# The sums of a mixture of experts: rows added in DRAM, or carried to their tokens by TensorE

## The chip, the cores and the metric

The kernel runs on one core of a Trainium2 chip. The metric is the device time of one execution in microseconds (us). Engines are named as in the profile: PE is TensorE, DVE is VectorE, ACT is ScalarE, POOL is GpSimd, and SP issues most of the transfers. SBUF is the working memory on the chip, PSUM holds the sums of PE in banks of 128 x 512 float32, and DRAM lies outside.

## What is computed

One decoder block for 512 tokens of 1024 channels, all in float32. A layer norm, two parallel token mixers and a second layer norm give `h`. Then each token is sent to the 4 of 32 experts that its router scores highest. The last part of the reference, cut:

```
top_logit, top_e = lax.top_k(h @ w_router + b_router, 4)
top_w = softmax(top_logit)
# for each token t and each of its four experts e:
hgu  = h[t] @ w_gate_up[e] + b_gate_up[e]            # 1024 x 2048
gate = minimum(hgu[:1024], 7); up = clip(hgu[1024:], -7, 7)
act  = (up + 1) * gate * sigmoid(1.702 * gate)
y[t] += top_w * (act @ w_down[e] + b_down[e])        # 1024 x 1024
ple = sigmoid(h @ w_ple_gate) * (p @ w_ple_proj)
out = layer_norm(2 ** 0.25 * h + y + ple)
```

The sum `2 ** 0.25 * h + y + ple`, a table of 512 x 1024 float32 (2 MB), is what the change is about.

## The kernel before

The mixers and the output projection come first. Their products are F32R (float32 in a single pass), each value split into a high and a low part, three products for one (`split_parts`, `mm3`, lines 168 to 184). From about 670 us on the experts run.

The experts are sorted on the chip by how many tokens chose them. Experts at odd places from 7 on are **short**, with 64 slots; the others are **long**, with 64 + 32 slots (`BLOCKS`, `IS_SHORT`, line 45). That makes 13 short and 19 long ones. An expert's weights are 12 loads of 1 MB: eight for gate and up, four for down. `unit` (line 1311) puts the loads into a ring of 18 tiles of 1 MB, made of buffers that the mixers no longer need. Two of the 18 are the two halves of `hr`, which holds `h` after the second norm. SP issues the loads; a load waits until PE has used the tile's last content.

In `expert` (line 1454) PE multiplies the gathered tokens by the weights as float32 products (two records each in the trace). The tokens are the stationary side: 64 slots fill half of the columns of the array, 32 slots a quarter. So `products` (line 1442) issues two or four products side by side, which write to different partitions of one bank, as a "block" whose row of partitions holds a half or a quarter of the channels. `pg` takes gate and up of the first 64 slots, `pq` of the other 32; four of the eight input pieces are held back (`LATE`) so that the gating on ACT and DVE (lines 1500 to 1504) runs beside the rest. The results are transposed (`turned`) and multiplied by the down weights into `po` and `pq`.

**Sums.** `y_d` is a table in DRAM. `scaled_rows` (line 1237) writes `2 ** 0.25 * h` into it by way of a tile `tmp`; the sort of the experts uses a tile of the same tag (line 1130). At the end of each expert ACT multiplies `po` and `pq` by the slots' weights into `og` (line 1587), and POOL issues one or two indirect transfers that add the rows to `y_d` at the slots' tokens (line 1596). The embedding term is worked out in 32 pieces of 128 tokens by 128 channels, one or two in each expert (`embed`, line 1024); after each four, POOL issues a transfer of 256 KB that adds them to `y_d` (line 1044).

**The end.** The last expert is short; its table is filled up so that all its 64 slots hold a token, and the rows of these tokens are finished apart from the others. While its weights are used, SP reads all of `y_d` back into four tiles (`fetch_rows`, line 1358), which waits for all adds, and POOL reads the last expert's own rows into `yr` (line 1402). The fourth load of its down weights is held behind `fetch_rows` (line 1570). `norm_steps` (line 1371) norms the four tiles in small steps between the products; two of them are finished on POOL. The last expert's own rows get their sum from `po` on DVE and their norm in `last_rows` (line 1411), and are written over the output by an indirect transfer.

The order of instructions on each engine is made by a planner from the program's order, with some pairs kept as written (`keep_in_program_order`) and some loads held back (`issue_after`). Short sums and transposes share four PSUM banks (tag `att`); `pg` and `pq` of the up products use four others.

Of the kernel before, what the change touches and what calls it, by code (L numbers as in the profile page):

```python
# [14 lines left out]
U8 = mybir.dt.uint8  # L15
AF = mybir.ActivationFunctionType
ALU = mybir.AluOpType
# [49 lines left out]
FETCH_AT = 3  # L67
# [28 lines left out]
def block_kernel(ctx: ExitStack, tc: tile.TileContext, a: dict, out: bass.AP):  # L96
# [704 lines left out]
    row_add = rtc.tile([P, 4], F32, name="row_add")  # L801
    key = rtc.tile([P, NE], F32, name="key")
# [8 lines left out]
    def routing_setup():  # L811
# [6 lines left out]

        v_.memset(row_add, 0.0)
# [61 lines left out]
    def table_rows(pool, ohs, ne, gi, si, parts):  # L881
        rows_from(pool, picked(pool, ohs, ne, lambda n, e: ids[:, n, :], 3), gi, si, parts)
# [8 lines left out]
    def tables(pool, e0, ne, base, gi, si, ws, places):  # L891
        ohs = pool.tile([P, NT, ne, P], BF16, name="ohs", tag="ohs")
        for n in range(NT):
            one_hot_slots(ohs, n, e0, ne, base, places)
        table_rows(pool, ohs, ne, gi, si, False)
        table_weights(pool, ohs, e0, ne, 1, ws)
# [127 lines left out]
    def embed(i):  # L1024
# [18 lines left out]
        if n == NT - 1:  # L1043
            nc.gpsimd.dma_start(y_d[:S, cs].rearrange("(n q) c -> q n c", q=P), emb["out"], accum_op=ALU.add)
# [125 lines left out]
    def first_tables():  # L1170
# [14 lines left out]
        table_rows(rtc, ohs0, 4, pair(gidx, 0), pair(sidx, 0), True)  # L1185
# [15 lines left out]
    def main_tables(e0):  # L1201
# [10 lines left out]
        weights_from(tb[:, :, 3:], pair(wslot, e0))  # L1212

# [94 lines left out]
    units += [hr[:, 2 * i:2 * i + 2, :].rearrange("p j d -> p (j d)") for i in range(2)]  # L1308
# [49 lines left out]
    def fetch_rows():  # L1358
        for n in range(NT):
            fetched = nc.sync.dma_start(yts[n], y_d[n * P:(n + 1) * P, :])  # L1360
        return fetched

# [8 lines left out]
    def norm_steps():  # L1371
        got = {}

        def first(n):
            mean, rs = got[n] = row_stats(ep, yts[n], keep=keep, bufs=NT + 1)
# [4 lines left out]
        def second(n):  # L1380
            if n in POOL_ROWS:
                shift, rs = got[n]
                keep(s_.activation(yts[n], yts[n], AF.Identity, scale=rs, bias=shift))
                g_.tensor_tensor(yts[n], yts[n], gb3, op=ALU.mult)
                g_.tensor_tensor(yts[n], yts[n], lasts["bias"], op=ALU.add)
            else:
                normed(yts[n], yts[n], got[n], gb3, lasts["bias"], keep)
# [66 lines left out]
    def expert(e):  # L1454
# [52 lines left out]
        down_order = (0, 2, 1, 3) if last else range(4)  # L1507
        if last:

            raws = [unit(rows_up(k)) for k in range(KD)]  # L1510
            raws_down = [unit(rows_down(u)) for u in down_order[:FETCH_AT]]
            yr = rows_to_add_to(e)
            fetched = fetch_rows()
            norm_steps()
        late = []
        for k in range(KD):
# [4 lines left out]
            raw = raws[k] if last else unit(rows_up(k))  # L1521
# [30 lines left out]
        if e == NE - 1:  # L1552
            spread(lasts["bias"], a["ln_moe_b"][0])

# [4 lines left out]
        if not last:  # L1559
            turned(sgs, as_, (more or [first])[0], range(2) if more else range(2, 4), True)  # L1560
# [3 lines left out]
        for i, u in enumerate(down_order):  # L1564
            if not last:
                raw = unit(rows_down(u))
            elif i < FETCH_AT:
                raw = raws_down[i]
            else:
                with tc.issue_after(fetched.ins):  # L1570
                    raw = unit(rows_down(u))
            if last and i == 1:
                turned(sgs, as_, first, range(2, 4), True)
# [107 lines left out]
```

## Time and profile before

| | us |
|---|---|
| median of three runs | 1806.24 |
| lowest and highest | 1805.43 to 1811.08 |
| the profiled execution | 1799.9 |
| its span, first to last instruction | 1798.2 |
| PE busy in the span | 1722.1 (96%) |
| DVE, ACT, POOL busy | 557.7, 409.5, 196.6 |
| mean granted PE clock | 0.985 of full |

The profile is of one execution, so its rows add up to its own time and not to the median. Busy time of PE is made of records whose ends are modelled: several products can run side by side, and a record can lie over the next one. What counts is how far starts lie from each other. A wait in a row stands in brackets: how long the engine was idle before it, and what released it.

### The profile page before, as it was taken

What the parts mean: (1) busy time and instruction counts of PE and PEld (TensorE: products, weight loads), DVE (VectorE), ACT (ScalarE), POOL (GpSimd) and SP (SyncE); (2) the same over time, 40 slices, a digit from 0 to 9 for tenths busy, and PEclk for the clock granted to TensorE, in tenths of its full rate; (3) what the DMA queues carried; (4) which work ended last, traced back from release to release, by engine and by line L of the source; (5) the groups of instructions that cost most, each with busy time, mean ns of one, the idle gap of its engine ahead of it and who ended that gap; (6) DMA issues with size and microseconds to landing.
All of it is one profiled execution on the core that took longest, in us unless ns stands there. A gap on an engine that the chain in (4) does not pass through costs nothing. (4 is left out here: it accounts for less than half of the span.)

```text
span 1798.2 us, 26077 instructions
## 1 busy us (share of the span) xinstructions
PE 1722.1 (96%) x10591; PEld 985.3 (55%) x10591; DVE 557.7 (31%) x1326; ACT 409.5 (23%) x653; POOL 196.6 (11%) x202
## 2 busy tenths in 40 slices
PE   6999999999998999999999999999999999999994
PEld 5888887788886873334334543443443443434422
DVE  7566455436344654102112112112111111112004
ACT  3665355234322321011110101111111011001111
POOL 1000000000000101111111110110110111110113
PEclk9999999999999999999999999999999999999997
DMA  8322233322217487999999999999999999999993
GB/s 268 106 71 71 71 132 103 141 94 71 94 71 288 168 332 283 370 366 387 364 342 361 412 408 384 405 411 386 406 412 372 405 412 371 405 385 413 404 355 133
DMA packets 127642, 513.93 MB, mean 286 GB/s; under 512 B 14434, under 2 KB 44546, under 8 KB 78228
## 3 DMA queue, kind: packets, MB, share of 16 engines
q1 hardware_dynamic: 95988, 466.11, 64.8%
q0 software_dynamic: 16160, 29.63, 6.8%
q10 hardware_dynamic: 15360, 16.39, 2.7%
q8 instruction: 86, 1.41, 0.3%
q14 instruction: 48, 0.39, 0.1%
HBM read 484.36 MB, written 27.72 MB: 285 GB/s over the span
## 5 line engine op out<-in xcount | busy, mean ns | idle before, releaser
L1452 PE MATMUL pg<-raw,turned 128*64 128x512 f32 (+1 forms) x2120 | 424.9, 533 | 6.1 <-DVE up L1502 3.7
L1452 PEld LDWEIGHTS pg<-raw,turned 128*64 128x64 f32 x2120 | 162.1, 137 | 227.5 <-issue 178.4
L1502 DVE TENSOR_SCALAR up<-pg 128x256 f32<-128x256 f32 (+1 forms) x45 | 24.2, 537 | 732.1 <-PE pg L1452 732.1
L1452 PE MATMUL pq<-raw,turned 128*32 128x512 f32 (+1 forms) x2000 | 192.1, 498 | 0.0
L1452 PE MATMUL po<-raw,turned 128*64 128x512 f32 x784 | 178.4, 604 | 0.0
L182 PE MATMUL proj<-H,parts_w 128*128 128x512 f32 x640 | 157.4, 394 | 3.4 <-ACT vt L499 2.0
L182 PE MATMUL proj<-parts_w,H 128*128 128x512 f32 x640 | 159.7, 394 | 0.0
L174 DVE TENSOR_TENSOR parts_w<-raw,parts_w 128x1024 fp32r<-128x1024 f32 x84 | 102.5, 1222 | 153.0 <-ACT parts_w L172 152.5
L1500 ACT ACTIVATE sgs<-pg 128x256 f32<-128x256 f32 (+1 forms) x45 | 21.3, 474 | 544.9 <-PE pg L1452 544.9
L182 PEld LDWEIGHTS proj<-H,parts_w 128*128 128x128 f32 x640 | 119.1, 188 | 28.3 <-ACT vt L499 2.4
L182 PEld LDWEIGHTS proj<-parts_w,H 128*128 128x128 f32 x640 | 120.1, 189 | 24.8 <-DVE H L939 0.3
L1596 POOL DMA_INDIRECT y_d<-og,sidx x50 | 80.3, 1605 | 455.8 <-ACT og L1587 260.3
L172 ACT ACTIVATE parts_w<-raw 128x1024 fp32r<-128x1024 f32 x84 | 88.7, 1059 | 177.4 <-PE proj L184 158.0
L1452 PEld LDWEIGHTS pq<-raw,turned 128*32 128x32 f32 x2000 | 54.8, 109 | 120.0 <-issue 101.7
L1452 PEld LDWEIGHTS po<-raw,turned 128*64 128x64 f32 x784 | 55.8, 140 | 99.3 <-issue 96.1
L1326 POOL DMA_INDIRECT xg<-h_d,gidx x49 | 50.6, 1032 | 393.4 <-PE ptr L1342 346.2
L184 PE MATMUL proj<-parts_w,H 128*128 128x512 f32 x320 | 83.5, 391 | 0.0
L184 PE MATMUL proj<-H,parts_w 128*128 128x512 f32 x320 | 80.5, 390 | 0.0
L1587 ACT ACTIVATE og<-po,wslot 128x512 f32<-128x512 f32 x32 | 22.0, 687 | 213.8 <-PE po L1452 213.8
L184 PEld LDWEIGHTS proj<-parts_w,H 128*128 128x128 f32 x320 | 60.3, 189 | 12.6
L184 PEld LDWEIGHTS proj<-H,parts_w 128*128 128x128 f32 x320 | 59.9, 188 | 12.4
L1037 PE MATMUL ple<-rawg,H 128*128 128x128 f32 x512 | 62.4, 275 | 0.0
(351 smaller groups left out, 1808.1 us busy)
## 6 DMA issues: line engine op xcount, KB each, us to landing
raw<-in_w_gate_up_dram SPq DMA_DIRECT2D x223, 1024.0 KB, 19.8
raw<-in_w_down_dram SPq DMA_DIRECT2D x98, 1024.0 KB, 19.4
raw<-in_w_in_dram SPq DMA_DIRECT2D x36, 1024.0 KB, 4.9
hr<-in_w_gate_up_dram SPq DMA_DIRECT2D x22, 1024.0 KB, 20.1
hr<-in_w_down_dram SPq DMA_DIRECT2D x20, 1024.0 KB, 19.5
gb<-in_w_gate_up_dram SPq DMA_DIRECT2D x11, 1024.0 KB, 19.7
gb<-in_w_down_dram SPq DMA_DIRECT2D x10, 1024.0 KB, 20.1
raw<-in_w_proj_a_dram SPq DMA_DIRECT2D x4, 1024.0 KB, 5.2
```

The source lines that it names most:

```text
L172: s_.activation(hi, src, AF.Copy)
L174: v_.tensor_tensor(lo, src, f32(hi), op=ALU.subtract)
L182: t_.matmul(ps, wh if keep else x, x if keep else wh, start=st, stop=False)
L184: t_.matmul(ps, wl if keep else xh, xh if keep else wl, start=False, stop=stop)
L1037: t_.matmul(pg[:, :P], H2[:, k, t], emb["gate"][:, k, :], start=(k == 0), stop=(k == KD - 1))
L1326: g_.indirect_dma_start(out=columns_of(xg, i), out_offset=None, in_=by_parts(h2_d, parts), in_offset=bass.IndirectOffsetOnAxis(ap=gidx[:, ...
L1452: t_.matmul(dst, x, cols, start=start, stop=stop, skip_group_check=closed)
L1500: s_.activation(dst, gate, AF.Sigmoid, scale=SW_ALPHA)
L1502: v_.tensor_scalar(tmp, up, LIMIT + 1.0, 1.0 - LIMIT, op0=ALU.min, op1=ALU.max)
L1587: s_.activation(columns_of(og, i), (po, pq)[i][:, :D // parts] if i else po, AF.Copy, scale=wslot[:, e, i:i + 1])
L1596: g_.indirect_dma_start(out=by_parts(y_d, parts), out_offset=rows_of(e, i), in_=columns_of(og, i), in_offset=None, compute_op=ALU.add)
```

## The change

`y_d` is no longer used in the main path. `hr` keeps the sums: it is scaled in place, the embedding's pieces are added to it by DVE, and each expert's weighted rows are carried to their tokens by PE. For that `tokens_held` makes, with the tables, the token number of each slot (`holds`; three columns, one for the first 64 slots and two for the other 32, of which each is valid in one half of the partitions). `weighted` splits the weighted rows into a high and a low part. `add` compares a row of token numbers with `holds` into `mine`, a matrix of slots by tokens, and multiplies it by both parts, with 64 slots in each half of the partitions. DVE adds the four sums to `hr`. The two halves of this work (256 tokens each) are queued in `waiting` and taken up in the next expert, behind the second and the fourth piece of its up products.

The ring of weights has 16 tiles, since `hr` is in use. In the last expert `fetch_rows` is gone, the norms read `hr`, its loads are issued in the ordinary order, and `yr` is picked from `hr` by a float32 product with a choice matrix. The scratch space of POOL's transfers is set to 8192 bytes. The path for overfull experts, which these inputs don't take, writes `hr` to `y_d` first.

```diff
+    holds = rtc.tile([P, NE, 3], F32, name="holds")
+    skip = rtc.tile([P, 2], F32, name="skip")
+    token_i = rtc.tile([P, S], I16, name="token_i")
...
+    def tokens_held(tb, e0):
+        hd = rtc.tile([P, 4], F32, name="hd")
+        v_.tensor_tensor(hd, tb[:, :, 0], tb[:, :, 1], op=ALU.add)
+        v_.scalar_tensor_tensor(hd, tb[:, :, 2], 2.0 * S, hd, op0=ALU.mult, op1=ALU.add)
+        hv = hd.rearrange("p (e i) -> p e i", i=2)
+        v_.tensor_scalar(holds[:, e0:e0 + 2, 0], hv[:, :, 0], -2.0 * S, None, op0=ALU.add)
+        for i in range(2):
+            v_.tensor_scalar(holds[:, e0:e0 + 2, 1 + i], hv[:, :, 1], skip[:, i:i + 1], -2.0 * S, op0=ALU.add, op1=ALU.add)
...
         v_.tensor_tensor(dst, pg[:, P:2 * P], dst, op=ALU.mult)
-        if n == NT - 1:
-            nc.gpsimd.dma_start(y_d[:S, cs].rearrange("(n q) c -> q n c", q=P), emb["out"], accum_op=ALU.add)
+        v_.tensor_tensor(hr[:, n, cs], hr[:, n, cs], dst, op=ALU.add)
...
         for n in range(NT):
-            tmp = ep.tile([P, D], F32, name="tmp", tag="og")
-            s_.activation(tmp, hr[:, n, :], AF.Copy, scale=ALPHA)
-            nc.scalar.dma_start(y_d[n * P:(n + 1) * P, :], tmp)
-        nc.scalar.dma_start(y_d[S:], hr[:, 0, :])
+            s_.activation(hr[:, n, :], hr[:, n, :], AF.Copy, scale=ALPHA)
...
-    units += [hr[:, 2 * i:2 * i + 2, :].rearrange("p j d -> p (j d)") for i in range(2)]
...
     def rows_to_add_to(e):
-        yr = ep.tile([P, D // 2], F32, name="yr", tag="xg")
-        g_.indirect_dma_start(out=yr, out_offset=None, in_=by_parts(y_d, 2), in_offset=rows_of(e, 0))
+        both = ep.tile([P, D], F32, name="yr", tag="xg")
+        yr, oh = both[:, :D // 2], both[:, D // 2:D // 2 + NT * SHORT_CAP].rearrange("p (n m) -> p n m", n=NT)
+        py = psm.tile([P, 512], F32, name="py", tag="att")
+        for n in range(NT):
+            v_.tensor_scalar(oh[:, n, :], iota_s[:, :SHORT_CAP], place1[:, n, e:e + 1], None, op0=ALU.is_equal)
+        for n in range(NT):
+            for j in range(2):
+                t_.matmul(py[j * SHORT_CAP:(j + 1) * SHORT_CAP, :], oh[:, n, :], hr[:, n, j * 512:(j + 1) * 512],
+                          start=(n == 0), stop=(n == NT - 1))
+        s_.activation(yr, py, AF.Copy)
         return yr
+
+    waiting = []
+
+    def weighted(e, sums):
+        parts = ep.tile([P, 2, D // 2 + D // 4], F32R, name="weighted", tag="og")
+        for (i, _, n, m), ps in zip(blocks(e), sums):
+            w, ps = wslot[:, e, i:i + 1], ps[:, :D // m]
+            hi, lo = (columns_of(parts[:, j], i) for j in range(2))
+            s_.activation(hi, ps, AF.Copy, scale=w)
+            v_.scalar_tensor_tensor(lo, ps, w, f32(hi), op0=ALU.mult, op1=ALU.subtract)
+
+        def add(half):
+            mine = ep.tile([P, 3, 2 * P], F32R, name="mine", tag="mine")
+            what = [(0, slice(0, 512), slice(0, 512))]
+            if not IS_SHORT[e]:
+                what += [(1 + j, slice(512, 768), slice(j * 256, j * 256 + 256)) for j in range(2)]
+            for c, _, _ in what:
+                v_.tensor_scalar(mine[:, c, :], token_i[:, half * 2 * P:(half + 1) * 2 * P], holds[:, e, c:c + 1], None,
+                                 op0=ALU.is_equal)
+            for i in range(2):
+                n = 2 * half + i
+                sums = [psm.tile([P, 512], F32, name="added", tag="att") for j in range(2)]
+                todo = [(c, src, dst, part) for c, src, dst in what for part in range(2)]
+                for x, (c, src, dst, part) in enumerate(todo):
+                    for j in range(2):
+                        r = slice(j * 64, (j + 1) * 64)
+                        t_.matmul(sums[j][:, dst], mine[r, c, i * P:(i + 1) * P], parts[r, part, src],
+                                  start=x == 0, stop=x == len(todo) - 1)
+                for j in range(2):
+                    cs = slice(j * 512, (j + 1) * 512)
+                    v_.tensor_tensor(hr[:, n, cs], hr[:, n, cs], sums[j], op=ALU.add)
+
+        waiting.extend([lambda: add(0), lambda: add(1)])
...
             if k < KD - LATE:
                 up(k, raw)
+                if k % 2 and waiting:
+                    waiting.pop(0)()
...
-        og = ep.tile([P, D // 2 + D // 4], F32, name="og", tag="og")
-        for i, _, n, parts in blocks(e):
-            s_.activation(columns_of(og, i), (po, pq)[i][:, :D // parts] if i else po, AF.Copy, scale=wslot[:, e, i:i + 1])
...
-        for i, _, n, parts in blocks(e):
-            g_.indirect_dma_start(out=by_parts(y_d, parts), out_offset=rows_of(e, i), in_=columns_of(og, i), in_offset=None,
-                                  compute_op=ALU.add)
+        if not last:
+            weighted(e, [po, pq] if more else [po])
+            return None
...
-    nc = bacc.Bacc("TRN2", target_bir_lowering=False, num_devices=1)
+    nc = bacc.Bacc("TRN2", target_bir_lowering=False, num_devices=1, dynamic_dma_scratch_size=8192)
```

## Rows read from the trace of the kernel before

**Rows 1.** The page: busy us (share of the span) xinstructions; the DMA share by slice.

```profile
PE 1722.1 (96%) x10591; PEld 985.3 (55%) x10591; DVE 557.7 (31%) x1326; ACT 409.5 (23%) x653; POOL 196.6 (11%) x202
...
DMA  8322233322217487999999999999999999999993
```

**Rows 2.** Stretches: us, each engine's busy us, granted clock, DMA share, GB/s.

```profile
704.00:1756.00 1052.00, 1033.77 (x7245) 438.74 (x7246) 161.34 (x500) 115.09 (x256) 139.34 (x106) 0.99 0.99 386
...
676.00:684.00 8.00, 5.49 (x26) 1.41 (x26) 7.90 (x20) 0.00 (x0) 0.00 (x0) 0.79 0.63 262
1541.90:1548.70 6.80, 6.01 (x28) 3.23 (x30) 1.33 (x3) 0.38 (x1) 0.00 (x0) 0.50 1.04 400
```

**Rows 3.** Timeline of ACT: the first output of experts 14 to 16 (start, us).

```profile
1194.23 0.69 ACT L1587 ACTIVATE og<-po,wslot 128x512 f32<-128x512 f32 x1 [6.88 <-PE po L1452]
...
1223.88 0.69 ACT L1587 ACTIVATE og<-po,wslot 128x512 f32<-128x512 f32 x1 [6.88 <-PE po L1452]
...
1260.45 0.69 ACT L1587 ACTIVATE og<-po,wslot 128x512 f32<-128x512 f32 x1 [6.88 <-PE po L1452]
```

**Rows 4.** Timeline of PE in the up products of long expert 16.

```profile
1231.32 1.94 PE L1452 MATMUL pg<-raw,turned 128*64 128x512 f32 x8
1233.18 1.06 PE L1452 MATMUL pq<-raw,turned 128*32 128x512 f32 x8
1234.18 1.94 PE L1452 MATMUL pg<-gb,turned 128*64 128x512 f32 x8
```

**Rows 5.** Waits of PE from 704 to 1756 us: total, times, longest.

```profile
PE ptr L1342 <- DVE sgs L1504: 10.4, 10, 1.0
PE pg L1452 <- DVE up L1502: 5.3, 10, 0.5
PE pg L1452 <- DMA raw<-in_w_gate_up_dram: 2.4, 2, 1.4
```

**Rows 6.** Timeline of PE in the output projection, F32R products.

```profile
648.58 1.07 PE L182 MATMUL proj<-parts_w,H 128*128 128x512 f32 x4
649.49 0.61 PE L184 MATMUL proj<-parts_w,H 128*128 128x512 f32 x2
649.94 1.07 PE L182 MATMUL proj<-parts_w,H 128*128 128x512 f32 x4
```

**Rows 7.** Timeline of PE in expert 14: embedding, then down products.

```profile
1184.30 1.95 PE L1037 MATMUL ple<-rawg,H 128*128 128x128 f32 x16
1186.08 0.61 PE L1039 MATMUL ple<-rawp,pT 128*128 128x128 f32 x4
...
1190.53 3.60 PE L1452 MATMUL po<-hr,turned 128*64 128x512 f32 x16
```

**Rows 8.** DMA from 704 to 1756 us: a queue's packets, MB, share; issues.

```profile
q0 software_dynamic: 14640, 22.81, 9.8%
...
y_d<-stg POOLq DMA_DIRECT2D x8, 256.0 KB, 8.8
...
y_d<-og,sidx POOLq DMA_INDIRECT x50, 9.4
```

**Rows 9.** DVE: a sum into hr by its line; a product by form.

```profile
L1067 DVE SCALAR_TENSOR_TENSOR hr<-hr,proj x8: 680/683/687, 612.5 to 652.2; 128x512 f32<-128x512 f32 x8
...
L1503 DVE SCALAR_TENSOR_TENSOR sgs<-sgs,sig_cap,up 128x512 f32<-128x512 f32 x18 | 13.5, 752 | 1.9
```

**Rows 10.** Timelines of DVE and PE in the first expert.

```profile
675.26 1.22 DVE L1133 TENSOR_TENSOR tmp<-key 128x1024 f32<-128x1024 f32 x1 [5.90 <-DMA y_d<-tmp]
...
678.51 0.18 PE L1143 MATMUL pord<-sel_by,facts 32*1 32x32 bf16 x1 [3.64 <-DVE sel_by L1141]
```

**Rows 11.** Timeline of PE in expert 25.

```profile
1539.67 1.08 PE L1452 MATMUL pg<-raw,turned 128*64 128x256 f32 x8 [0.94 <-DMA raw<-in_w_gate_up_dram]
1542.17 1.97 PE L1452 MATMUL pg<-raw,turned 128*64 128x256 f32 x8 [1.41 <-DMA raw<-in_w_gate_up_dram]
```

**Rows 12.** Timeline of PE in the last expert, the second bias row.

```profile
1762.82 2.82 PE L161 MATMUL pbr<-bb,ones_f 1*128 1x512 f32 x4 [1.10 <-DMA bb<-in_ln_moe_b_dram]
```

More of the change, by code (lines that the diff above doesn't have):

```diff
@@ L15 @@
 U8 = mybir.dt.uint8
+I16 = mybir.dt.int16
 AF = mybir.ActivationFunctionType
@@ L817, in routing_setup @@
         v_.tensor_scalar(dump, pcol, float(S), None, op0=ALU.add)
+        g_.iota(token_i, pattern=[[1, S]], base=0, channel_multiplier=0, allow_small_or_imprecise_dtypes=True)
+        v_.memset(skip, 0.0)
+        n = BLOCKS[1][1]
+        for j in range(P // n):
+            v_.memset(skip[j * n:(j + 1) * n, (j + 1) % 2:(j + 1) % 2 + 1], -2.0 * S)
         v_.memset(row_add, 0.0)
@@ L894, in tables @@
             one_hot_slots(ohs, n, e0, ne, base, places)
-        table_rows(pool, ohs, ne, gi, si, False)
+        rows_from(pool, picked(pool, ohs, ne, lambda n, e: ids[:, n, :], 3), gi, si, False)
         table_weights(pool, ohs, e0, ne, 1, ws)
@@ L1184, in first_tables @@
         block_slots(ohs0, 0)
-        table_rows(rtc, ohs0, 4, pair(gidx, 0), pair(sidx, 0), True)
+        tb = picked(rtc, ohs0, 4, lambda n, e: ids[:, n, :], 3)
+        rows_from(rtc, tb, pair(gidx, 0), pair(sidx, 0), True)
+        tokens_held(tb, 0)
         v_.tensor_tensor(ex, top[:, :, :TOPK], top[:, :, 0:1].to_broadcast([P, NT, TOPK]), op=ALU.subtract)
@@ L1374, in first @@
         def first(n):
-            mean, rs = got[n] = row_stats(ep, yts[n], keep=keep, bufs=NT + 1)
+            mean, rs = got[n] = row_stats(ep, hr[:, n, :], keep=keep, bufs=NT + 1)
             if n in POOL_ROWS:
@@ L1382, in second @@
                 shift, rs = got[n]
-                keep(s_.activation(yts[n], yts[n], AF.Identity, scale=rs, bias=shift))
+                keep(s_.activation(yts[n], hr[:, n, :], AF.Identity, scale=rs, bias=shift))
                 g_.tensor_tensor(yts[n], yts[n], gb3, op=ALU.mult)
@@ L1386, in second @@
             else:
-                normed(yts[n], yts[n], got[n], gb3, lasts["bias"], keep)
+                normed(yts[n], hr[:, n, :], got[n], gb3, lasts["bias"], keep)
             nc.sync.dma_start(out[n * P:(n + 1) * P, :], yts[n])
@@ L1506, in expert @@
         last = e == NE - 1
-        down_order = (0, 2, 1, 3) if last else range(4)
         if last:
[L1510 to L1513, printed above, removed]
             norm_steps()
@@ L1520, in expert @@
                 main_tables(2)
-            raw = raws[k] if last else unit(rows_up(k))
+            raw = unit(rows_up(k))
             late.append((k, raw))
@@ L1557, in expert @@
             done.append(e)
-        if not last:
-            turned(sgs, as_, (more or [first])[0], range(2) if more else range(2, 4), True)
+        turned(sgs, as_, (more or [first])[0], range(2) if more else range(2, 4), True)
         po = psm.tile([P, 512], F32, name="po", tag="att")
@@ L1563, in expert @@
         todo = []
[L1564 to L1573, printed above, removed]
+        for u in range(4):
+            raw = unit(rows_down(u))
             for h in range(2):
-                products(first, po, tokens(as_, 2 * u + h, first), raw[:, h:h + 1, :], stop=i == 3 and h == 1)
+                products(first, po, tokens(as_, 2 * u + h, first), raw[:, h:h + 1, :], stop=u == 3 and h == 1)
                 take_step()
@@ L1612, in block_kernel @@
         og = expert(e)
+    most = nc.values_load(over[0:1, 0:1], min_val=0, max_val=S)
+    with tc.If(most > 0):
+        for n in range(NT):
+            nc.sync.dma_start(y_d[n * P:(n + 1) * P, :], hr[:, n, :])
+        g_.indirect_dma_start(out=by_parts(y_d, 2), out_offset=bass.IndirectOffsetOnAxis(ap=sidx[:, NE - 1, 0:1], axis=0),
+                              in_=og, in_offset=None, compute_op=ALU.add)
     moe2.close()
@@ L1617, in block_kernel @@
     plx.close()
-    most = nc.values_load(over[0:1, 0:1], min_val=0, max_val=S)
     gi_d = dram.tile([NE, P], I32, name="gi_d")
@@ L1622, in block_kernel @@
     with tc.If(most > 0):
-        g_.indirect_dma_start(out=by_parts(y_d, 2), out_offset=bass.IndirectOffsetOnAxis(ap=sidx[:, NE - 1, 0:1], axis=0),
-                              in_=og[:, :D // 2], in_offset=None, compute_op=ALU.add)
         with tc.tile_pool(name="ovc", bufs=1, side="left") as oc:
```

24 lines of the change are left out of this document (10 added, 14 removed).

## The prediction

> **What bounds the kernel now.** I began with the page's busy shares and its slices. TensorE (PE) is busy for 96% of the span, and the DMA engines are at 9 tenths or more from the eighteenth slice on [rows 1]. Two resources stand at their limit, and the change takes work from one (DMA) and gives work to the other (PE). So the first question is which of them paces the experts, from about 704 to 1756 us. The table of stretches gives PE 1033.8 of 1052.0 us there, so 18.2 us idle, and a DMA share of 0.99 [rows 2]. A full share does not decide it, because the loads of weights run ahead through a ring and take whatever time there is. The cadence decides. In the timeline of ACT the first sum of each expert's output starts at 1194.23, 1223.88 and 1260.45: 29.65 us for a short expert (64 slots) and 36.57 us for a long one (96 slots) [rows 3]. A queue of equal 12 MB loads would give equal steps; these follow the number of slots, which is PE work. In the timeline of PE eight records on pg and eight on pq follow each other every 2.86 us, without a gap [rows 4]. Each float32 product is two records. Eight pairs on po, 16 records, take 3.60 us with the last one's end, some 0.43 us for records that run side by side [rows 7]. Four pairs and two sets of four are then 6 x 0.43 = 2.58 us, so the array streams nearly all the time; the other 0.28 us is two changes between column tilings. The list of waits agrees: of the idle time 2.4 us is put down to a landing of weights, 10.4 and 5.3 us to the gating on VectorE (DVE) [rows 5]. The experts are bound by PE. DMA is a close second: once, at 1539 to 1549 us, PE does run out of weights [rows 11].
>
> **What the change adds on PE.** For each of 31 experts it sends two parts (high and low) of the weighted rows through a choice matrix of 64 rows by 128 tokens. These are F32R products, for four token tiles and two halves of 64 slots. A short expert has 4 x 2 x 2 = 16 products over 512 columns. A long one has these and 4 x 2 x 2 x 2 = 32 over 256 columns. There are 12 short ones (7, 9, ... 29; the last one is left out) and 19 long ones, so 19 x 48 + 12 x 16 = 1104 products. Nothing is taken from PE, which excludes a gain by these instructions themselves.
>
> The price of one: the projections are F32R products of 128 rows by 512 columns. Six of them start in 649.94 - 648.58 = 1.36 us, so 0.227 us each, with the load of their 128 weight columns hidden [rows 6]. How a load of 128 columns bounds a shorter product is seen in the embedding's gate: 16 float32 records of 128 columns in 1186.08 - 1184.30 = 1.78 us, 0.111 us each [rows 7]. The two halves of 64 rows are issued one after the other, to different banks. No row shows such halves. As the column halves of rows 4 run side by side, I take it that these do too. Then a pair over 512 columns takes 0.227 us, and a pair over 256 columns needs 0.114 us of streaming but two loads, 2 x 0.111 = 0.222 us. I take 0.227 us for either pair, since the nearest row with a load for each product is the load-bound one.
> - Long: 24 pairs x 0.227 = 5.45 us; x 19 = 103.5 us. Short: 8 pairs x 0.227 = 1.82 us; x 12 = 21.8 us. Sum **125.3 us**.
> - The ends: with loads overlapped too, a 256-column pair takes 0.114 us, long 3.64 us, sum 91 us. With nothing overlapped and every product at 0.227 us, long 10.9, short 3.63 us, sum 251 us.
> - The products come in two blocks for each expert, in the middle of the next one's up products, each with a change of tiling before and behind it: 4 x 0.14 = 0.56 us; x 31 = **17.4 us** (ends 0, if they fall where a change is anyway, and 35 if a row tiling costs double).
> - The last expert's rows to add to are picked by eight float32 products of 128x512. Eight such calls, 16 records, take 3.6 us in the row of po [rows 7]. Some of it fills the 1.1 us in which PE waits for the last bias row [rows 12]: **+2.3 us** (ends 0 and 3.6).
>
> **What it adds elsewhere.** DVE gets, for a long expert, eight sums over 128x512 at 0.68, two low parts at 0.75 or less, and six one-hot tables of 128x256, which I price at the 0.75 of the wider row as an upper end [rows 9]: at most 11.4 us in an expert of 36.6 us, where DVE is busy 161 of 1052 us [rows 2]. ACT writes the high part in place of the weighted rows. PE's cover is the next expert's up products, over ten us between the second block and the gating. If the sums stood ahead of the gating in DVE's queue, PE would wait one to two sums, 0.7 to 1.4 us, in each expert: 21 to 42 us. I take 0 and keep it for the range. The products of the first block wait for the low part, 0.75 us behind the high one on DVE; two rows of up products (3.4 us) stand ahead of them, so 0. Four banks serve po, pq, the transposes and now the sums; a block takes all four, and DVE frees them in 4 x 0.68 = 2.7 us, less than the 3.4 us of products to the next block: 0.
>
> **What it removes.** The adds in DRAM go: 50 indirect ones and eight of 256 KB by the embedding [rows 8]. By size they are 31 x 0.262 + 19 x 0.131 + 8 x 0.262 = 12.7 MB of the 22.81 MB on the software queue, which takes 9.8% of 1052 us, so about 57 us of DMA time. PE does not wait for them, so it is worth what PE lost to late weights: 0.94 and 1.41 us of waiting [rows 11], and behind that 6.8 us at half clock (0.50 granted, the level of 1.2 GHz) [rows 2], of which half is lost: **-5.8 us**. At the start of the first expert, the sort of the experts on DVE waits 5.90 us for a store of the scaled rows, and PE 3.64 us behind it [rows 10]. In 676 to 684 us the mean granted clock is 0.79, and I put that at 1.7 us more: **-5.3 us**. The ring of weights loses two of 18 tiles, 2.1 MB, 5.4 us of lead at 386 GB/s; with PE taking 66.2 + 5.45 + 1.82 + 1.1 = 74.6 us for two experts and DMA less than before, the lead is never used up: 0. In the tail the reads of the rows from DRAM go (four of 512 KB); the end hangs on the last expert's output and its norm, which stay: 0 (ends -3, if the norms of the other rows start earlier and POOL is free sooner, and +3).
>
> **Sum.** 125.3 + 17.4 + 2.3 - 5.8 - 5.3 = +133.9 us. The profiled execution took 1799.9 us for a span of 1798.2; the median of the runs shown is 1806.24, 6.3 above it. 1799.9 + 133.9 + 6.3 = **1940 us**.
>
> **Rivals.**
> - The halves of 64 rows do not run side by side. For it: no row here shows row halves. Against it: column halves do. Then a 512-column product is 0.227 and a 256-column one 0.12 us, long 16 x 0.227 + 32 x 0.12 = 7.47, short 3.63: 185.5 us in place of 125.3, **2000 us**.
> - The loads of the two halves overlap as well, 91 us in place of 125.3: **1906 us**. For it: the four loads of 32 columns on pq hide in rows 4. Against it: those are short ones. The Trainium skill, TensorEngine Tiling, section Tiling Modes, says that tiles load weights and multiply in parallel; by that rule it would be this rival and not the one above, and no row of this trace has row tiles to show it.
> - PE's clock falls in the blocks. It fell to 0.50 behind waits, in stretches of 6.8 us, each worth 3.4 us; one for each of 31 experts gives +106: **2046 us**. Against it: the blocks hold no wait.
> - The other side: DMA paces the experts. Its share is 0.99 and it has a dry spot; if every pair of experts waited for its weights, the 57 us would come back and PE's additions lie inside the loads, 1806 - 57 - 5 = **1744 us**. It decides from the point at which PE's own work for two experts is below what DMA needs: 66.2 us of DMA at full share, less 57/16 = 3.6, so 62.6 us. Against it: PE's 66.2 us are dense and would be 74.6.
>
> **How the numbers follow.** 0.62 for the forecast (its own range 1915 to 1975: no price for the tilings, or 31 us of delayed gating), 0.16 for serial halves, 0.13 for overlapped loads, 0.04 for the clock, 0.03 for DMA, 0.02 for other gains that I don't see. The range of 1885 to 2015 takes in the first three with their spread and leaves out the clock, DMA, and serial halves with loads in the open. A difference of 0.3% is about what a measurement of this kernel can tell from none. Faster 0.04 (DMA and half of the rest), same 0.01, slower 0.95.
>
> **What would show it.** In the changed profile: the outputs of a short and a long expert 66 us apart before should be some 75 us apart; the new products should stand in PE's timeline with starts about 0.11 us apart in the mean; the DMA share in the experts should fall to about 0.85 and SP should wait for PE to free tiles; no wait of DVE for a store near 675 us. It is wrong if two experts still take 66 us or less, if the new products fill gaps that PE had, or if their mean start-to-start is near 0.06 or above 0.2 us.

## The result, and the profile after

The changed kernel takes 1866.26 us (median; 1862.80 to 1872.66, 4 runs) against 1805.84 for the kernel before; over all runs it takes 1.0346 times as long, with a 95% interval of [1.0322, 1.0369]. The forecast was 1940 us in a range from 1885 to 2015. The sign was right, the size too large: +60 us, not +134. The profiled executions give +68.4 us of span (1866.6 against 1798.2) and are what the rows below are read from.

The page and the table of stretches of the kernel after (engine, busy us, share, instructions; DMA share by slice; then the stretch of the experts with each engine's busy us, granted clock, DMA share, GB/s):

```profile
PE 1812.2 (97%) x11711; PEld 1083.4 (58%) x11711; DVE 791.5 (42%) x1883; ACT 410.5 (22%) x654; POOL 101.0 (5%) x144
...
DMA  7312233322236568878889989989989989988861
```

```profile
704.00:1820.00 1116.00, 1114.86 (x8296) 530.22 (x8297) 393.93 (x1040) 115.08 (x256) 44.58 (x48) 1.00 0.88 355
```

Against [rows 1, 2]: TensorE (PE) is now busy for all but 1.1 us of 1116 at full clock, where it had 18 us idle; the DMA share fell from 0.99 to 0.88, close to the 0.85 of the forecast. VectorE (DVE) went from 161 to 394 us, and no product of PE waits for it there.

The outputs of experts 14 to 16 in ACT's timeline (start, us), the answer to [rows 3]:

```profile
1240.28 0.69 ACT L1432 ACTIVATE weighted<-po,wslot 128x512 fp32r<-128x512 f32 x1 [6.83 <-PE po L1506]
1274.42 0.69 ACT L1432 ACTIVATE weighted<-po,wslot 128x512 fp32r<-128x512 f32 x1 [6.89 <-PE po L1506]
1309.99 0.69 ACT L1432 ACTIVATE weighted<-po,wslot 128x512 fp32r<-128x512 f32 x1 [6.83 <-PE po L1506]
```

The short expert's step is 34.14 us (29.65 before), the long one's 35.57 (36.57 before): 69.7 us for the two instead of 66.2, where the forecast said 75. The long expert became shorter although it carries two blocks of the new products. The timeline of PE shows both reasons. In the first part (short expert 15) the two blocks of products for the rows of long expert 14 stand, in the second (long expert 16) those for expert 15:

```profile
1248.41 2.14 PE L1451 MATMUL added<-weighted,mine 64*128 64x512 f32 x24
1250.48 3.65 PE L1506 MATMUL pg<-raw,turned 128*64 128x512 f32 x16
1254.07 2.14 PE L1451 MATMUL added<-weighted,mine 64*128 64x512 f32 x24
1256.14 3.67 PE L1506 MATMUL pg<-raw,turned 128*64 128x256 f32 x32
...
1275.76 3.83 PE L1506 MATMUL pg<-raw,turned 128*64 128x512 f32 x16
1279.52 1.21 PE L1451 MATMUL added<-weighted,mine 64*128 64x512 f32 x8
1280.65 3.65 PE L1506 MATMUL pg<-raw,turned 128*64 128x512 f32 x16
1284.24 1.19 PE L1451 MATMUL added<-weighted,mine 64*128 64x512 f32 x8
1285.36 3.64 PE L1506 MATMUL pq<-raw,turned 128*32 128x512 f32 x32
1288.93 7.09 PE L1506 MATMUL pg<-raw,turned 128*64 128x512 f32 x32
1295.95 3.64 PE L1506 MATMUL pq<-raw,turned 128*32 128x512 f32 x32
1299.52 0.75 PE L1357 MATMUL ptr<-ident,sgs 128*128 128x128 f32 x4
```

First, a block is cheap: from its first product to the next other product 2.07 us for 24 products (1248.41 to 1250.48) and 1.13 us for 8 (1279.52 to 1280.65). All 62 blocks together, 38 of the one kind and 24 of the other, take 106.4 us; the forecast had 142.7. Second, pg and pq no longer alternate as in [rows 4]: four pieces of pg (32 records), then four of pq. Eight pieces cost 2.86 us each in the alternating order; here a run of four pieces on pg and pq takes 7.02 + 3.57 = 10.6 us (1288.93 to 1295.95 to 1299.52), 2.65 a piece. The planner put the ten long experts from 12 to 30 into this order; in the kernel before only the early ones had it.

### The profile page after: what moved, and what is told of

Same layout as the page of the kernel before. It is cut to its first block, busy times and chain, and to the rows that moved or that the text cites. A ratio compares the mean times of both kernels' runs of the same rounds, so it can differ in the third digit from the quotient of the medians.

```text
span 1866.6 us, 28743 instructions
## 1 busy us (share of the span) xinstructions
PE 1812.2 (97%) x11711; PEld 1083.4 (58%) x11711; DVE 791.5 (42%) x1883; ACT 410.5 (22%) x654; POOL 101.0 (5%) x144
## 5 line engine op out<-in xcount | busy, mean ns | idle before, releaser
L1506 PE MATMUL pg<-raw,turned 128*64 128x512 f32 (+1 forms) x2336 | 448.8, 523 | 3.5 <-DVE up L1556 2.4
L1506 PEld LDWEIGHTS pg<-raw,turned 128*64 128x64 f32 x2336 | 184.4, 137 | 211.6 <-issue 147.7
L1455 DVE TENSOR_TENSOR hr<-hr,added 128x512 f32<-128x512 f32 x248 | 153.8, 681 | 177.7 <-PE added L1451 177.7
L1506 PE MATMUL po<-raw,turned 128*64 128x512 f32 x960 | 211.3, 592 | 0.0
L1506 PE MATMUL pq<-raw,turned 128*32 128x256 f32 (+1 forms) x2336 | 201.3, 485 | 0.0
L182 PEld LDWEIGHTS proj<-H,parts_w 128*128 128x128 f32 x640 | 119.1, 188 | 28.0 <-ACT vt L499 2.2
L1506 PEld LDWEIGHTS pq<-raw,turned 128*32 128x32 f32 x2336 | 69.9, 109 | 108.5 <-issue 83.3
L1451 PEld LDWEIGHTS added<-weighted,mine 64*128 64x128 f32 x1104 | 83.6, 185 | 59.1 <-issue 50.3
L1451 PE MATMUL added<-weighted,mine 64*128 64x512 f32 (+1 forms) x1104 | 110.8, 340 | 0.0
L1433 DVE SCALAR_TENSOR_TENSOR weighted<-po,wslot,weighted 128x512 fp32r<-128x512 f32 x31 | 23.3, 750 | 185.1 <-ACT weighted L1432 185.1
```

The costliest lines, as they stand in the source:

```text
L182: t_.matmul(ps, wh if keep else x, x if keep else wh, start=st, stop=False)
L1433: v_.scalar_tensor_tensor(lo, ps, w, f32(hi), op0=ALU.mult, op1=ALU.subtract)
L1451: t_.matmul(sums[j][:, dst], mine[r, c, i * P:(i + 1) * P], parts[r, part, src], start=x == 0, stop=x == len(todo) - 1)
L1455: v_.tensor_tensor(hr[:, n, cs], hr[:, n, cs], sums[j], op=ALU.add)
L1506: t_.matmul(dst, x, cols, start=start, stop=stop, skip_group_check=closed)
```

## Experiments

"Grouped" means here that the up products of the long experts from 12 on are pinned in the written order (pg of four pieces, then pq of four), which is the one that the planner gives them in the changed kernel.

**1. The kernel before, grouped.** Only the pins, in `products`:

```
-            t_.matmul(dst, x, cols, start=start, stop=stop, skip_group_check=closed)
+            made = t_.matmul(dst, x, cols, start=start, stop=stop, skip_group_check=closed)
+            if pin and j == 0:
+                keep(made)
```

> The kernel before, with one thing changed: in the long experts from 12 on the up products stand in the program's order (pg of four pieces, then pq of four), as the planner put them in the changed kernel; before, it alternated pg and pq piece by piece there (36.6 us for such an expert, 33.2 us for experts 8 and 10, which it had not alternated). Theory 1, PE alone paces these experts: ten of them get 3.4 us shorter, 1806 - 34 = about 1772 us. Theory 2, DMA was just as late as PE (its share is 1.01 there), so that the order cost nothing: at most 8 us shorter, 1798 to 1806, with PE now waiting for weights.

Measured: 1801.42 us (1798.01 to 1807.95), ratio 0.999 [0.9973, 1.0007]: the order by itself is worth 5 us at most, and perhaps nothing. Two waits of PE from 704 us on and the stretch from 930 to 1560 us in this run (waiter, releaser, total, times, longest; then columns as above):

```profile
PE pg L1452 <- DMA raw<-in_w_gate_up_dram: 25.1, 17, 3.0
PE pbr L161 <- DMA bb<-in_ln_moe_b_dram: 8.1, 1, 8.1
```

```profile
930.00:1560.00 630.00, 604.93 (x4306) 280.19 (x4304) 102.70 (x322) 67.28 (x153) 82.48 (x63) 1.00 1.00 393
```

PE now runs out of weights 17 times, against 2 in [rows 5], at a DMA share of 1.00. At the output of expert 30 the run is 10.1 us ahead of the kernel before (1733.64 against 1743.75), but in the last expert PE waits 8.1 us for the transfer of a bias row, 1.1 in [rows 12].

Four pairs of experts use 96 loads, 100.66 MB. What the queue of the loads moved between the outputs of experts 16 and 24, in the kernel before (four pairs of 66.23 us) and in this run (of 68.04 us); packets, MB, share:

```profile
q1 hardware_dynamic: 13381, 97.47, 89.0%
q1 hardware_dynamic: 13821, 100.64, 89.5%
```

In this run the loads move just as much as is used, and PE waits for them: 68.0 us a pair is what DMA needs with all adds in DRAM. PE needed 66.23 in the kernel before, and there the loads moved 3.2 MB less than was used. So DMA was 1.8 us a pair too slow already, and the ring's lead hid it until the dry spot in expert 25 [rows 11].

**2. The changed kernel without the products and sums, grouped.**

```
-        waiting.extend([lambda: add(0), lambda: add(1)])
```

> The changed kernel without the products that carry the rows and without their sums (the experts' part of the output is left out except for the last expert's), with the up products in the grouped order. Both theories: the changed kernel's 62 blocks take 106 us of PE's timeline. If they cost just that, 1866 - 106 = 1760 us; this is also what the freed DMA and the order are worth together without their price. If DMA paces at this speed even without the adds in DRAM, or if the blocks filled gaps, it is higher: 1775 or more.

Measured: 1755.06 us (1746.11 to 1756.57), ratio 0.9716 [0.968, 0.9753]; 63.1 us a pair. The change therefore costs 1866.26 - 1755.06 = 111 us for its products and sums, 106 of them seen as blocks in PE's timeline, and gives back 49 us.

**3. The changed kernel, alternating.** The pins are set so that pg and pq follow each other piece by piece, as in the kernel before.

```
+                if pinned:
+                    up_more(k, raw)
+                    late = []
```

> The changed kernel with the up products of the long experts from 12 on alternating between pg and pq, as in the kernel before. If the order is what gave the 3.4 us in each of ten long experts back: 1866 + 34 = 1900 us. If these experts got shorter for another reason (weights that land earlier), it stays at 1866.

Measured: 1898.83 us (1898.41 to 1899.42), ratio 1.053 [1.0502, 1.0558], 32.6 us more than the changed kernel. In PE's timeline the 2.86 us a piece of [rows 4] are back:

```profile
1291.57 1.94 PE L1506 MATMUL pg<-raw,turned 128*64 128x512 f32 x8
1293.44 1.06 PE L1506 MATMUL pq<-raw,turned 128*32 128x512 f32 x8
1294.43 1.94 PE L1506 MATMUL pg<-raw,turned 128*64 128x512 f32 x8
```

In the two traces the order is worth less than 32.6 us: from the first output of expert 0 to that of expert 31 this run takes 1161.4 us and the changed kernel 1135.3, which is 26.1 us, and 4.7 us of the difference between the profiled executions lie ahead of the experts, in code that the edit does not touch. From expert 14 to 24 a pair takes 72.34 us instead of 69.80. Of these 2.5 us, 8 x 0.21 = 1.7 are changes between tile shapes, and 0.8 is gating for which PE waits again, as in [rows 5]:

```profile
PE ptr L1357 <- DVE sgs L1560: 8.3, 10, 0.8
```

**4. The two row halves in turn.** All products of one half of 64 rows are queued ahead of those of the other.

```
-                for x, (c, src, dst, part) in enumerate(todo):
-                    for j in range(2):
+                for j in range(2):
+                    for x, (c, src, dst, part) in enumerate(todo):
```

> The changed kernel with the products of the first half of 64 rows all ahead of those of the second half, in each token tile, so that neighbours in PE's queue lie in the same rows. If two halves run side by side only as neighbours, a 512-column product costs 0.235 and a 256-column one 0.115 us each: short blocks +0.94 us (24), long ones +1.86 us (38), 93 us together, 1959 us. If PE works on the halves independently of the order, it stays at 1866.

Measured: 1894.24 us (1890.57 to 1897.32), ratio 1.0502 [1.047, 1.0535]. Rows of PE around a block of either kind:

```profile
1229.11 1.22 PE L1451 MATMUL added<-weighted,mine 64*128 64x512 f32 x8
1230.26 2.33 PE L1506 MATMUL pq<-raw,turned 128*32 128x512 f32 x17
...
1263.01 2.93 PE L1451 MATMUL added<-weighted,mine 64*128 64x512 f32 x24
1265.87 3.65 PE L1506 MATMUL pg<-raw,turned 128*64 128x512 f32 x16
```

The 38 long blocks take 2.87 us in the mean instead of 2.07, which makes 30 us, against the 28 us by which the time is longer; the short ones, with two products of one half ahead of two of the other, stay at 1.14. So the halves do run side by side in the changed kernel (that rival of the forecast falls), but my expectation of the full loss, 93 us, was wrong too: TensorE overlaps halves that stand two products apart in its queue without loss, and those six apart in part. The planner is not the reason: the program of this run has the products in the written order, six of one half and six of the other in each long block, two and two in each short one. In the long block at 1263.01 us, whose 24 records are all there, these products had started by 1263.60 (count, then busy us and mean ns):

```profile
L1451 PE MATMUL added<-weighted,mine 64*128 64x512 f32 x3 | 1.1, 461 | 0.0
L1451 PE MATMUL added<-weighted,mine 64*128 64x256 f32 x1 | 0.3, 273 | 0.0
```

A half begins with two products over 512 columns and goes on with four over 256. The third one over 512 columns is the first of the other half, and it started while three products that stand ahead of it in the queue had not.

**5. The high part alone.** The low part's products are left out, grouped order.

```
-                todo = [(c, src, dst, part) for c, src, dst in what for part in range(2)]
+                todo = [(c, src, dst, 0) for c, src, dst in what]
```

> The changed kernel with the high part of the weighted rows alone (the low part's products are left out, the rest stays, up products of long experts in grouped order): half of the add products. Theory (a block's price is its pairs of products, 0.235 us for 512 columns and 0.115 us for 256, the rest fixed): a short expert's block 1.13 - 0.47 = 0.66 us, a long one's 2.07 - 0.93 = 1.14 us, 24 and 38 of them 59 us instead of 106; time 1866 - 47 = 1819 us. Rival (the price is mostly fixed: tiling changes and waits for VectorE's choice matrices): blocks of 0.95 and 1.7 us, time about 1847 us.

Measured: 1840.45 us (1836.95 to 1842.95), ratio 1.0195 [1.0169, 1.0221]. The blocks are as the theory has them, the time is not. PE in a long expert where the block is whole, and in a later one where the planner spread it:

```profile
1191.81 0.73 PE L1451 MATMUL added<-weighted,mine 64*128 64x512 f32 x4
1192.47 3.65 PE L1506 MATMUL pg<-raw,turned 128*64 128x512 f32 x16
...
1257.06 0.50 PE L1451 MATMUL added<-weighted,mine 64*128 64x512 f32 x2
1257.48 1.94 PE L1506 MATMUL pg<-raw,turned 128*64 128x512 f32 x8
1259.35 0.50 PE L1451 MATMUL added<-weighted,mine 64*128 64x512 f32 x2
```

Four products take 0.66 us and eight 1.13, so a pair over 512 columns costs 0.235 us and 0.19 us are fixed. The long block then gives (2.07 - 1.13) / 8 = 0.117 us for a pair over 256 columns. All blocks are 61.4 us here (59 expected). The 21 us that are missing lie largely in the order: the five long experts from 16 to 24, with their runs of two products and of eight records on pg, take 36.5 us where 34.6 were due (9 us), and expert 30 loses another 4.7. The rest is spread thinly.

**6 and 7. The kernel before without its adds in DRAM**, alternating and grouped. Together with experiment 1 they make a table of two causes.

```
-        for i, _, n, parts in blocks(e):
-            g_.indirect_dma_start(out=by_parts(y_d, parts), out_offset=rows_of(e, i), in_=columns_of(og, i), in_offset=None,
-                                  compute_op=ALU.add)
...
-            nc.gpsimd.dma_start(y_d[:S, cs].rearrange("(n q) c -> q n c", q=P), emb["out"], accum_op=ALU.add)
```

> The kernel before without any add into DRAM (the experts' 50 and the embedding's); the sums of the experts and of the embedding are left out, the order of TensorE's products stays the alternating one. Theory (two coupled limits: TensorE in the alternating order needs 36.6 us for a long expert from 12 on, and DMA was as late): taking the DMA load away alone is worth little, a pair stays at 36.6 + 29.7 us, span within 1 to 8 us of before: 1790 to 1802 us. Rival (DMA alone paced the kernel before, the order costs nothing): the pair falls to 63 us and the time to about 1755 us, as in the run without products. A DMA share near 0.93 with no idle time of TensorE would support the theory.

> As the run before it (no adds into DRAM, their sums left out), but with the up products of the long experts from 12 on in grouped order. Theory (both limits must go together): about 1757 us, pair 63 us, that is some 40 us less than the run with the alternating order, although the grouped order alone was worth 2 us in the kernel before. Rival (order worth nothing at all, DMA the only limit): the same time as the run with the alternating order. Third (the prediction's own term, DMA relief 5.8 us): 1795 us.

Measured, medians in us:

| | alternating | grouped |
|---|---|---|
| adds in DRAM | 1803.3 | 1801.4 |
| no adds | 1799.7 [ratio 0.9957, 0.9992] | 1763.3 [ratio 0.9748, 0.9806] |

Either alone is worth 2 to 4 us, both together 40. The stretch from 930 to 1560 us of the two runs without adds (alternating, then grouped):

```profile
930.00:1560.00 630.00, 618.30 (x4312) 273.67 (x4310) 102.06 (x322) 67.28 (x153) 27.41 (x29) 1.00 0.95 390
```

```profile
930.00:1560.00 630.00, 625.59 (x4458) 291.66 (x4460) 105.00 (x339) 69.98 (x159) 28.34 (x30) 1.00 0.97 399
```

The queue of the adds and gathers between the outputs of experts 16 and 24 in experiment 1 (adds, grouped), then the queue of the loads and that queue in experiment 7 (no adds, grouped):

```profile
q0 software_dynamic: 3616, 5.77, 9.3%
```

```profile
q1 hardware_dynamic: 13600, 99.08, 94.5%
q0 software_dynamic: 832, 2.62, 2.7%
```

With the adds gone and the old order, DMA has 5% of its time to spare and a pair still takes 66.5 us. With the new order it takes 63.25 us; PE does not wait for weights, but the loads move 99.08 of the 100.66 MB that are used, so the lead still shrinks. From that I estimate that DMA needs 63.25 x 100.66 / 99.08 = 64.3 us a pair without adds, and that the adds took 68.0 - 64.3 = some 3.8 us of it. The run in the alternating order also shows that taking the adds out of DRAM does not by itself make the planner group the products.

**8 to 10. Part of the rows each way.** Every kernel here keeps the embedding's sums in SBUF and the grouped order; the rows of long experts are added in DRAM again, in a buffer that starts at zero and is fetched in the last expert. By TensorE go the rows of no expert, of every second short one (as in the diff), or of all short ones.

```
-        if not last:
+        if not last and (e % 4 == 3 and IS_SHORT[e]):
             weighted(e, [po, pq] if more else [po])
             return None
+        if not last:
...
+            for n in range(NT):
+                g_.dma_start(yts[n], y_d[n * P:(n + 1) * P, :])
+            for n in range(NT):
+                keep(v_.tensor_tensor(hr[:, n, :], hr[:, n, :], yts[n], op=ALU.add))
             norm_steps()
```

> The changed kernel with no add products at all: every expert's rows are added in DRAM as before (into rows that start at zero and are fetched and added to the sums in SBUF in the last expert); only the embedding's 8 adds stay in SBUF, up products of long experts from 12 on grouped. Theory (DMA and TensorE were both at 66.2 us a pair; without any adds DMA is busy 61.4 us a pair, so the adds, 640 KB of experts' rows and 128 KB of the embedding a pair, take 4.8 us of it): DMA paces at 65.4 us a pair, some 9 us and the dry spot near expert 25 (5 us) gained, 4 us lost in the last expert: about 1793 us. Rival (the embedding's adds, issued early and off the queue of the loads, cost the loads nothing): 1803 us.

> As the run before it, but the rows of every second short expert (7, 11, 15, 19, 23, 27) go by TensorE into SBUF, the rest in DRAM. Theory: TensorE 63.25 + 1.13 = 64.4 us a pair in the mean, DMA 64.5 us: both limits meet, about 1784 us, the best of the three and faster than both kernels. Rival (what is saved is lost to the coupling: a pair with products is bound by TensorE, one without by DMA, and the ring of loads can't even them out): pairs of 65.5 and 65.4 us, about 1794 us.

> As the run before it, but the rows of all 12 short experts before the last go by TensorE into SBUF, those of the long ones in DRAM. Theory: TensorE 63.25 + 2.27 = 65.5 us a pair, DMA 63.4 us, so TensorE paces: about 1795 us. Rival (the planner goes back to other orders when products are added, each change of tile shape at 0.2 us): 1805 us or more.

Measured, with the ratio to the kernel before in brackets: 1808.68 us [1.001, 1.0036], 1798.70 us [0.9951, 0.9979] and 1811.87 us [1.0024, 1.0063]. All missed by 15 to 17 us, for one reason above all: the last expert. There DVE's four sums stood ahead of the gating in its queue and waited for the fetched rows, and PE waited for the gating (DVE, then PE, of the second kernel):

```profile
1748.79 1.23 DVE L1573 TENSOR_TENSOR hr<-hr,H 128x1024 f32<-128x1024 f32 x1 [23.61 <-DMA H<-y_d]
```

```profile
1760.12 5.95 PE L1511 MATMUL pg<-raw,turned 128*64 128x256 f32 x32 [18.97 <-DVE up L1563]
```

The pairs from expert 14 to 24 are 66.9, 65.6 and 67.05 us apart. The first waits for weights at a DMA share of 1.00; the last does not wait for weights at all, and is PE's own time, 1.5 us above the 65.5 expected. The planner broke its 24 blocks into 41 runs: the blocks of a long expert take 3.10 us there instead of 2.25, and where they stay whole (experts 8, 10, 26) the expert is 1.3 us shorter. The second has the least, as the two limits have it.

**11 and 12. The last expert mended**, for half of the short experts and for none.

```
-            for n in range(NT):
-                keep(v_.tensor_tensor(hr[:, n, :], hr[:, n, :], yts[n], op=ALU.add))
...
         def first(n):
+            keep(v_.tensor_tensor(hr[:, n, :], hr[:, n, :], yts[n], op=ALU.add))
             mean, rs = got[n] = row_stats(ep, hr[:, n, :], keep=keep, bufs=NT + 1)
...
-            yr = rows_to_add_to(e)
...
             take_step()
+        yr = rows_to_add_to(e)
```

> The kernel with the rows of every second short expert by TensorE, but in the last expert VectorE's four sums of the fetched rows stand behind its gating instead of ahead of it (ahead of it they held TensorE for 19 us), and the pick of the last expert's rows stands behind the down products. Theory: the distance between the outputs of experts 30 and 31 falls from 52.7 to about 36 us (32 in the kernel before, plus 4 for the pick), nothing else moves: 1798.7 - 16.7 = about 1782 us, faster than both kernels. Rival (the last expert is bound by its loads behind the fetched rows, not by the order on VectorE): 1795 us or more.

> The same mend of the last expert in the kernel that has only the embedding's sums in SBUF. Theory (DMA paces it, TensorE waits for weights 15 us in all): 57.0 to about 38 us in the last expert, 1808.7 - 19 = about 1790 us, that is 5 to 10 us above the kernel with half of the short experts by TensorE, since there both limits are lowered. Rival (what TensorE's products cost is all that counts, and fewer are better): at or below the other kernel's time.

Measured: 1780.25 us (1776.90 to 1786.05), ratio 0.9871 [0.9853, 0.9889], and 1787.37 us (1785.34 to 1792.88), ratio 0.9909 [0.9893, 0.9925], against 1782 and 1790 expected. PE's wait for the gating in the first of them, and its stretch from 704 us:

```profile
1733.53 3.86 PE L1512 MATMUL pg<-raw,turned 128*64 128x256 f32 x32 [0.53 <-DVE up L1564]
```

```profile
704.00:1760.00 1056.00, 1041.38 (x7402) 463.14 (x7398) 230.25 (x704) 121.75 (x266) 134.28 (x108) 1.00 0.97 384
```

Experts 30 and 31 are 34.9 and 37.1 us apart instead of 52.7 and 57.0. The kernel with half of the short experts' rows by TensorE, which also has the grouped order, beats the one before by 1.3% and the changed one by 4.6%.

## Why the prediction was wrong

In spans, the forecast was +133.9 us and the profile shows +68.4. The steps:

| step | forecast | measured |
|---|---|---|
| 62 blocks of products, with their changes of tiling | +142.7 | +106.4 |
| order of long experts' up products (experiment 3) | 0 | -26.1 |
| pick of the last expert's rows | +2.3 | +5.3 |
| longer wait for the gating in the last expert | 0 | +1.8 |
| wait for the last bias row, gone | (in the pick) | -1.1 |
| dry spot in expert 25 | -5.8 | -5.4 |
| sort stall in the first expert | -5.3 | -1.2 |
| two stretches at half clock of before | 0 | -6.8 |
| tail behind the last expert's output | 0 | -2.4 |

These leave -2 us that I can't assign. The two stretches at half clock (1.2 GHz), 3.4 us lost in each, stand in the trace of before and have no counterpart after, other than the 3.4 us counted in the pick:

```profile
1729.60:1736.40 6.80, 6.80 (x18) 1.94 (x18) 0.00 (x0) 2.72 (x5) 0.00 (x0) 0.50 1.01 423
1763.80:1770.60 6.80, 6.80 (x17) 1.79 (x17) 5.21 (x15) 2.77 (x5) 3.12 (x8) 0.50 0.11 48
```

Runs of one kernel differ in this too (mean granted clock 0.981 to 0.988 over the runs of the kernel before), so these 6.8 us can't be put down to the change.

**The step that failed first is the price of a pair over 256 columns**: "I take 0.227 us for either pair, since the nearest row with a load for each product is the load-bound one." It is 0.117 us, and a change of tiling 0.19 us a block and not 0.28 (experiment 5). The loads of the two halves overlap like their products. This was the second rival, at 1906 us, and it had a chance of 0.13 because I let a row with one load at a time [rows 7] speak for two that run side by side. The Trainium skill, TensorEngine Tiling, section Tiling Modes, says that tiles load weights and multiply in parallel; the 0.117 us agree with it (a load alone takes 0.111 us in [rows 7]).

**The second is that the order of the other products was taken as given**, and with it the freed DMA time: "it is worth what PE lost to late weights", 5.8 us. The reading that PE paced the experts was right, [rows 3] and [rows 4] say so, and experiment 6 bears it out: without adds in DRAM the time moves by 4 us. But a full DMA share was put aside as undecided. It hid a second limit, 1.8 us a pair above PE with the adds (68.0 against 66.2) and 1.9 below it without them (64.3), where the rival on DMA had it level with PE and 3.6 below. So a shorter order of PE's work was worth at most 5 us before and 36 us once the adds were gone (1799.7 to 1763.3; experiments 1, 6, 7). The changed kernel happened to bring that order (which part of the change made the planner choose it, no run shows): experiment 3 takes it away and the time is 1898.83 us. With the right prices for the pairs and no new order the forecast would have been about 1940 - 36 = 1904 us, and that run lies 5 us from it. So the price of the pairs alone would have left the time inside the range; the order took it out.

**Smaller terms.** The sort's wait went as said; PE goes straight on:

```profile
679.72 0.17 PE L1159 MATMUL pord<-sel_by,facts 32*1 32x32 bf16 x1
```

But 4 of the 5.3 us were given back just ahead of it, where the granted clock of a stretch fell to half (1.2 GHz) while PE was busy throughout:

```profile
662.80:676.50 13.70, 13.70 (x56) 8.92 (x57) 6.67 (x24) 4.26 (x6) 0.00 (x0) 0.51 0.82 344
```

In the kernel before the same stretch stood at 1.00. Nine of the ten profiles of kernels with the change, whole or in part, have such a stretch of 13.7 us between 662 and 682 us; that of experiment 11 does not, with PE busy throughout as well, and its first output comes 5.9 us earlier (705.43 against 711.30):

```profile
662.80:676.50 13.70, 13.70 (x90) 6.61 (x88) 10.36 (x29) 4.04 (x5) 0.00 (x0) 1.00 0.79 331
```

What brings it on was not tried. The pick and the longer wait in the last expert, PE:

```profile
1827.43 3.86 PE L1506 MATMUL pg<-raw,turned 128*64 128x256 f32 x32 [2.37 <-DVE up L1556]
1831.21 0.51 PE L1357 MATMUL ptr<-ident,sgs 128*128 128x128 f32 x2
1831.66 1.98 PE L161 MATMUL pbr<-bb,ones_f 1*128 1x512 f32 x4
1833.57 5.35 PE L1419 MATMUL py<-hr,yr 128*64 128x512 f32 x16
1838.85 0.51 PE L1357 MATMUL ptr<-ident,sgs 128*128 128x128 f32 x2
```

The pick takes 5.3 us, of which 3.4 at half clock, where the forecast had 2.3 added; and in the short last expert the gating does stand behind DVE's sums and the norm's statistics, 2.4 us instead of the 0.5 of [rows 5]. In all other experts the cover held: no wait of PE is listed from 704 to 1820 us, as forecast. The bulk on DVE was sized as it came out (a sum into hr 0.681 us, a low part 0.750, a choice matrix 0.345 against the 0.75 taken as the upper end). The remaining 8 us between 1940 and the time lie in the offset: the forecast put the median 6.3 us above the profiled execution, and after the change it lies 2.1 below it (1868.4).

## What to carry to other kernels

When two resources are both near full, find the need of each by itself before pricing a move from one to the other: take the one's work away and shorten the other's in separate runs, since either alone may show nothing while both together are worth 2%. A DMA share of 0.99 behind a ring of loads does not tell whether DMA keeps up; what it moved against what was used does (97.47 against 100.66 MB in four pairs). Then move only as much as levels the two: all of it cost 3.5% here; the embedding's sums and a part of the short experts' rows, with the shorter order, gained 1.3%.

And ask what a planner will do with the work around the edit: the same products in another order were worth 26 us in the traces (33 between the medians), and where it broke blocks into short runs, 21 of the 47 us that halving the products should have gained were not seen.

## What the runs showed of the hardware

- Two products on different halves of 64 rows cost 0.235 us for 512 columns and 0.117 us for 256, weight loads included, on top of 0.19 us for each change into this tiling and back (experiment 5).
- TensorE overlaps the halves even if they don't alternate in its queue (experiment 4): blocks with two products of one half ahead of two of the other lose nothing (1.14 against 1.13 us), those with six ahead of six take 2.87 us instead of 2.07. If products started strictly in the order of the queue, only the last of one run and the first of the next would overlap: the shorter block would take five times 0.235 us and 0.19, 1.37 us, and the longer one four runs of 0.94 us less three overlaps of 0.117 us, plus 0.19, 3.6 us. The Trainium skill, TensorE: Matmul & The Clock Gate, section Part 2: What happens when you issue a matmul, says that only weight loads are pulled ahead and products keep their order. Across row halves the two measured times speak against that, and so does the product over 512 columns that started ahead of three that stood before it in the queue.
- Adds into DRAM, 0.79 MB a pair of experts ((5.77 - 2.62) / 4), cost the loads beside them some 3.8 us (68.0 less 64.3, an estimate from experiments 1 and 7), near the 3.6 that the forecast took by bytes. The busy share of their queue says more: 9.3% of 68.04 us less 2.7% of 63.25, 4.6 us.
